# Interleaving the two token halves in the last output group of a decoder-layer kernel

## The chip, the cores and the metric

The kernel runs on one core of a Trainium2 chip. The metric is the device time of one execution in microseconds. The core has a matrix engine (TensorE, here PE), a vector engine (VectorE, DVE), a scalar engine (ScalarE, ACT), GpSimd (POOL), and SyncE (SP), which here issues transfers. Each engine takes its instructions in the order in which they stand in its own list, and waits at an instruction until the semaphores named there have their counts.

## The reference, cut to what matters

One residual layer over 256 tokens of width 2048: three token-mixer branches, each projected to the model width and merged by gates, then an output projection, the residual, and a final norm. The change is in the last line but one, in a quarter of its columns.

```python
merged = (g_sb * (o_sb @ w_branch_sb[layer])
          + g_ssd * (o_ssd @ w_branch_ssd[layer])
          + g_mem * (o_mem @ w_branch_mem[layer]))
x = x + merged @ w_out[layer]
return rms_norm(x, final_norm_w)     # x / sqrt(mean(x*x) + eps) * final_norm_w
```

## The kernel before

Float32 products are made of three reduced-precision ones: each operand is split into a high and a low part (`split`: ACT makes the high part, line 146; DVE subtracts to get the low part, line 150), and PE adds high x high, high x low and low x high into one accumulator in PSUM. Weights are streamed: `load_chunk` (line 207) has SP load two k-tiles of 128 rows x 512 columns (512 KB) into one of four `raw` buffers, `split` writes `wh` and `wl`, and the matmuls follow. Tokens are 256, in two halves `t` of 128; the halves are the two 128-column slices of the left operand.

The output projection has 2048 columns in four groups of 512, with 16 k-tiles each. Groups 0 to 2 go through `gemm` (lines 266 to 268), which takes both token halves for each k-tile, in an accumulator tile `acc` with one 512-column bank for each half. The tag `acc` has two buffers, taken in turn. What follows a group (`out_half`, line 880: residual add on DVE, then squares on ACT and a product on POOL) is deferred by three chunks of the next `gemm`, so that it doesn't hold up the splits. Group 2 has no `gemm` behind it.

Group 3, the last one, is written out by hand (lines 934 to 953). First its eight chunks are loaded and split into four `wlh` and four `wll` tiles that hold them all (`his`, `los`); then `drain()` issues what was still deferred, which is group 2's `out_half` for both halves; so these stand behind the eight splits on DVE. Then come the products: token half 0 with all 512 columns and 16 k-tiles; its epilogue `last_cols` (lines 892 to 898: residual add, squares, sum, norm weight, for 256 columns at a time) and `write_out` (lines 902 to 912: inverse root on POOL, scaling of the whole row on DVE and ACT, five writes); then token half 1 in two column halves of 256 with 16 k-tiles each, each in an accumulator of its own and each with its `last_cols`, and at the end `write_out`. Engines' lists are in the order of this code: no scheduler moves anything. Waits are derived from which tiles an instruction reads and writes; an accumulator buffer that is taken again waits for the readers of the tile that had it.

Of the kernel before, what the change touches and what calls it, by code (L numbers as in the profile page):

```python
# [10 lines left out]
F32 = mybir.dt.float32  # L11
# [5 lines left out]
P = 128  # L17
D = 2048
T = 256
NKT = D // P  # L20
GW = 512
# [4 lines left out]
LATE = 3  # L26
WARM = 10
LATE_C = 2
NEG = -1.0e30

SB_HEADS = 8
# [10 lines left out]
def trunk_kernel(  # L42
# [6 lines left out]
    nc = tc.nc  # L49
# [7 lines left out]
    psA = ctx.enter_context(tc.tile_pool(name="psA", bufs=2, space=bass.MemoryType.PSUM))  # L57
# [4 lines left out]
    def nm(s):  # L62
        cnt[0] += 1
        return f"{s}_{cnt[0]}"
# [13 lines left out]
    def tq(shape, n):  # L78
        return tmp.tile(shape, F32, tag="tq", name=nm(n), bufs=2)

    def small(shape, n="small"):
        return sm.tile(shape, F32, tag="small", name=nm(n), bufs=12)
# [4 lines left out]
    def bank(shape, n="bank"):  # L87
        return psB.tile(shape, F32, tag="bank", name=nm(n))
# [19 lines left out]
    def keep_warm(n):  # L108
        for _ in range(n):
# [9 lines left out]
    nc.gpsimd.memset(cmask, 0.0)  # L119
    nc.gpsimd.affine_select(out=smask, in_=cmask, compare_op=ALU.is_gt, fill=NEG, base=0,  # L120
                            pattern=[[1, P]], channel_multiplier=-1)
    nc.gpsimd.affine_select(out=cmask, in_=cmask, compare_op=ALU.is_ge, fill=NEG, base=0,
                            pattern=[[1, P]], channel_multiplier=-1)
# [48 lines left out]
    def defer(fn, chunks=LATE):  # L172

        cnt[0] += 1
        heapq.heappush(late, (now[0] + chunks, cnt[0], fn))
# [9 lines left out]
    def pump():  # L185


        now[0] += 1
        while late and late[0][0] <= now[0]:
            heapq.heappop(late)[2]()  # L190
        advance(lanes[now[0] % 2])
# [6 lines left out]
    def drain():  # L198
        while lanes[0] or lanes[1] or late:
            pump()  # L200
# [10 lines left out]
    def gemm_cols(lhs, nk, w, c0, evac, ready=None, acc=None):  # L211
# [7 lines left out]
        for k0 in range(0, nk, KCC):  # L219
# [16 lines left out]
            pump()  # L236
        defer(lambda: evac(acc), LATE_C)

# [201 lines left out]
    for g in range(4):  # L440
        gemm_cols(memT, NKT, w_mem_kv, 2 * g * P, to_split_cols(kT, 2 * g),
                  acc=None if g else [bank([P, 2, T], "acc") for _ in range(2)])
# [384 lines left out]
    mT = []  # L827
# [61 lines left out]
    def last_cols(t, cs, acc, xr):  # L889
        for c in range(cs.start, cs.stop, T):  # L890
            yc = yo[t][:, 3 * GW + c:3 * GW + c + T]
            nc.vector.tensor_tensor(yc, acc[:, c - cs.start:c - cs.start + T], xr[:, c:c + T],
                                    ALU.add)
            junk = tq([P, T], "junk")
            q = ssy[:, t, 3 + c // T:4 + c // T]
            nc.scalar.activation(junk, yc, AF.Square, scale=D ** -0.5, accum_out=q)
            nc.vector.tensor_tensor(msy[:, t:t + 1], q, msy[:, t:t + 1], ALU.add)
            nc.vector.tensor_tensor(yc, yc, fw[:, 3 * GW + c:3 * GW + c + T], ALU.mult)

    def write_out(t):  # L900
        rs = small([P, 1], "frs")
        nc.gpsimd.tensor_tensor(rs, msy[:, t:t + 1], mhalf[:, 0:1], ALU.pow)
        for c0, c1, eng, dma in ((0, 256, nc.vector, nc.sync), (256, 640, nc.scalar, nc.scalar),
                                 (640, 1152, nc.vector, nc.sync),
                                 (1152, 1536, nc.scalar, nc.scalar),
                                 (1536, 2048, nc.vector, nc.sync)):
            o = yo[t][:, c0:c1]
            if eng is nc.vector:
                eng.tensor_scalar(o, o, rs, None, ALU.mult)
            else:  # L910
                eng.activation(o, o, AF.Copy, scale=rs)
            dma.dma_start(out[t * P:(t + 1) * P, c0:c1], o)

    def x_chunk(g):
        xr = t4([P, 2, GW], "xr")
        nc.scalar.dma_start(
            xr, x[:, g * GW:(g + 1) * GW].rearrange("(t p) n -> p t n", p=P))
        return xr
# [9 lines left out]
        gemm(mT[0], NKT, w_out, g * GW, out_evac(g))  # L928


    g = 3
    xr = x_chunk(g)
    his, los = [], []
# [4 lines left out]
        raw = load_chunk(w_out, g * GW, GW, k0, KC)  # L938
        split((his[-1][:, k0 % 4:k0 % 4 + KC], los[-1][:, k0 % 4:k0 % 4 + KC], raw, None))
    drain()  # L940
    for t in range(2):
        tt = slice(t * P, (t + 1) * P)
        for cs in (slice(0, GW),) if t == 0 else (slice(0, T), slice(T, GW)):
            acc = psA.tile([P, 2, GW], F32, tag="acc", name=nm("acc"),
                           bufs=2)[:, 0, 0:cs.stop - cs.start]
            for kt in range(NKT):
                lh, ll = mT[0].at(kt)
                wh, wl = his[kt // 4][:, kt % 4, cs], los[kt // 4][:, kt % 4, cs]
                nc.tensor.matmul(acc, lh[:, tt], wh, start=(kt == 0), stop=False)
                nc.tensor.matmul(acc, lh[:, tt], wl, start=False, stop=False)  # L950
                nc.tensor.matmul(acc, ll[:, tt], wh, start=False, stop=(kt == NKT - 1))
            last_cols(t, cs, acc, xr[:, t])
        write_out(t)


_INS = ['x', 'mem', 'x_cols', 'mem_cols', 'w_cols', 'w_in', 'b_gate', 'dt_bias', 'a_log',
# [39 lines left out]
```

## Time and profile before

| | |
|---|---|
| median of 3 runs | 1229.85 us (1229.75 to 1230.08) |
| the profiled execution | 1229.11 us |
| its span, first to last instruction | 1227.3 us |
| mean granted PE clock | 0.999 |
| PE busy | 1215.8 us |
| PE's first matmul of group 3 | 1195.56 us |
| PE's last matmul ends | 1219.26 us |

In the rows a matmul's name is its accumulator and its operands (`acc<-wlh,mT`), with the moving operand's columns behind (512 or 256). A matmul's duration includes its way through the array and overlaps the next one's, so the rate is read from start to start. PEld are weight loads into the array, which run beside the matmuls.

### The profile page before, as it was taken

Reading aid. Unit: us, or ns where it says so; the run is one execution under the profiler, and the core shown is the slowest. Engines: PE = TensorE matmul, PEld = TensorE weight load, DVE = VectorE, ACT = ScalarE, POOL = GpSimd, SP = SyncE. Lnnn points to the kernel's source line nnn. Section 1 sums busy time; section 2 is a strip of 40 time slices with the busy share of each in tenths; the row PEclk is TensorE's granted clock in tenths of the full one; section 3 lists DMA queues with packets and bytes.
Section 4 is the critical chain, followed back from the end, with each engine's and each line's share of the span. In section 5 each row is a group of like instructions: output and inputs, shape, how many; then the busy total and the mean of one; then the engine's idle time right before and its main releaser. Section 6 shows DMA issues by size and latency. Waiting matters only on the chain.

```text
span 1227.3 us, 16568 instructions
## 1 busy us (share of the span) xinstructions
PE 1215.8 (99%) x6388; PEld 1034.4 (84%) x6388; DVE 784.0 (64%) x990; ACT 645.8 (53%) x873; POOL 51.9 (4%) x50
## 2 busy tenths in 40 slices
PE   9999999999999999999999999999999999999997
PEld 7888888888888888888888888888878888888886
DVE  5686554565654555888888758577677655555554
ACT  6765543554444454545665756484757544444443
POOL 0000000000000000010100000000000010110101
PEclk9999999999999999999999999999999999999999
DMA  9966566655566656565567666566756666567673
GB/s 341 335 199 189 162 196 189 185 169 164 168 178 184 188 172 180 169 184 173 176 185 228 207 197 215 183 218 189 232 183 189 206 191 210 186 198 240 199 244 110
DMA packets 175023, 242.70 MB, mean 198 GB/s; under 512 B 10272, under 2 KB 109792, under 8 KB 174816
## 3 DMA queue, kind: packets, MB, share of 16 engines
q1 hardware_dynamic: 168656, 230.17, 60.9%
q10 hardware_dynamic: 6288, 11.48, 2.7%
q8 instruction: 50, 0.82, 0.3%
q14 instruction: 29, 0.24, 0.1%
HBM read 239.48 MB, written 2.13 MB: 197 GB/s over the span
## 4 chain that ended last, share of the span: by engine, by line
PE 95%; DMA 1%; ACT 1%; DVE 1%; issue 1%; SPq 0%; POOLq 0%; POOL 0%; ACTq 0%
PE acc L229 29%; PE acc L266 15%; PE acc L233 14%; PE acc L267 14%; PE acc L268 14%; PE acc L401 1%; PE acc L402 1%; PE acc L400 1%; PE y L773 1%; DMA raw<-in_w_out_dram 1%; DMA raw<-in_w_mem_kv_dram 1%; DVE wl L150 0%; ACT wh L146 0%; PE dtp L460 0%; PE xp L731 0%
## 5 line engine op out<-in xcount | busy, mean ns | idle before, releaser
L150 DVE TENSOR_TENSOR wl<-raw,wh 128x1024 fp32r<-128x1024 f32 (+1 forms) x409 | 504.5, 1237 | 310.3 <-ACT wh L146 305.1
L146 ACT ACTIVATE wh<-raw 128x1024 fp32r<-128x1024 f32 (+1 forms) x409 | 431.1, 1055 | 390.9 <-PE acc L268 200.6
L229 PE MATMUL acc<-hT,wh 128*128 128x512 f32 x1408 | 444.0, 397 | 0.0
L233 PEld LDWEIGHTS acc<-hT,wl 128*128 128x128 f32 x1408 | 264.5, 188 | 62.5
L233 PE MATMUL acc<-hT,wl 128*128 128x256 f32 x1408 | 276.8, 278 | 0.0
L229 PEld LDWEIGHTS acc<-hT,wh 128*128 128x128 f32 x1408 | 214.4, 189 | 0.1
L266 PE MATMUL acc<-wh,hT 128*128 128x512 f32 x448 | 175.7, 392 | 0.0
L267 PE MATMUL acc<-wl,hT 128*128 128x512 f32 x448 | 174.6, 390 | 0.7 <-DVE wl L150 0.7
L268 PE MATMUL acc<-wh,hT 128*128 128x512 f32 x448 | 174.5, 390 | 0.0
L267 PEld LDWEIGHTS acc<-wl,hT 128*128 128x128 f32 x448 | 84.2, 188 | 18.1 <-DVE wl L150 1.2
L268 PEld LDWEIGHTS acc<-wh,hT 128*128 128x128 f32 x448 | 84.1, 188 | 17.7
L266 PEld LDWEIGHTS acc<-wh,hT 128*128 128x128 f32 x448 | 84.1, 188 | 17.6 <-issue 0.7
L266 PE MATMUL acc<-wh,oD 128*128 128x512 f32 x128 | 49.8, 389 | 0.0
L267 PE MATMUL acc<-wl,oD 128*128 128x512 f32 x128 | 49.8, 389 | 0.0
L268 PE MATMUL acc<-wh,oD 128*128 128x512 f32 x128 | 49.8, 389 | 0.0
L688 DVE SCALAR_TENSOR_TENSOR cT<-cu,wcols,cT 128x255 f32<-128x255 f32 (+2 forms) x96 | 46.4, 483 | 3.4
L853 POOL TENSOR_TENSOR merged<-merged,sig 128x512 f32<-128x512 f32 x16 | 24.9, 1574 | 522.6 <-DVE sig L852 522.6
L229 PE MATMUL acc<-memT,wh 128*128 128x512 f32 x128 | 40.6, 398 | 0.0
L266 PE MATMUL acc<-wh,mT 128*128 128x512 f32 x96 | 37.4, 390 | 0.0
L268 PE MATMUL acc<-wh,mT 128*128 128x512 f32 x96 | 37.4, 389 | 0.0
L267 PE MATMUL acc<-wl,mT 128*128 128x512 f32 x96 | 37.4, 389 | 0.0
L631 POOL TENSOR_TENSOR lm<-lm,sp 128x384 f32<-128x384 f32 x8 | 13.1, 1642 | 394.7 <-DVE sp L630 385.0
(250 smaller groups left out, 1298.8 us busy)
## 6 DMA issues: line engine op xcount, KB each, us to landing
raw<-in_w_in_dram SPq DMA_DIRECT2D x288, 512.0 KB, 3.8
raw<-in_w_branch_ssd_dram SPq DMA_DIRECT2D x32, 512.0 KB, 4.5
raw<-in_w_out_dram SPq DMA_DIRECT2D x32, 512.0 KB, 5.0
raw<-in_w_mem_kv_dram SPq DMA_DIRECT2D x31, 512.0 KB, 5.7
raw<-in_w_branch_mem_dram SPq DMA_DIRECT2D x16, 512.0 KB, 3.6
raw<-in_w_branch_sb_dram SPq DMA_DIRECT2D x16, 512.0 KB, 4.8
dec<-acT SPq DMA_DIRECT2D x24, 256.0 KB, 8.0
sig<-in_b_gate_dram ACTq DMA_DIRECT2D x12, 256.0 KB, 4.4
```

Of the source, the lines that this page charges most:

```text
L146: nc.scalar.activation(hi, src, AF.Copy, **({} if scale is None else {"scale": scale}))
L150: nc.vector.tensor_tensor(lo, src, h32, ALU.subtract)
L229: nc.tensor.matmul(halves[b], wh[:, kt - k0, b * P:(b + 1) * P], lhs.both(kt), start=first, stop=False, skip_group_check=True)
L233: nc.tensor.matmul(halves[b][:, 1], wl[:, kt - k0, b * P:(b + 1) * P], lhs.at(kt)[0], start=False, stop=last, skip_group_check=True)
L266: nc.tensor.matmul(a, lh[:, tt], wh[:, j], start=first, stop=False)
L267: nc.tensor.matmul(a, lh[:, tt], wl[:, j], start=False, stop=False)
L268: nc.tensor.matmul(a, ll[:, tt], wh[:, j], start=False, stop=last)
L400: nc.tensor.matmul(a, lh[:, tt], wh[:, g], start=first, stop=False)
L401: nc.tensor.matmul(a, lh[:, tt], wl[:, g], start=False, stop=False)
L631: nc.gpsimd.tensor_tensor(lm, lm, sp, ALU.subtract)
L688: nc.vector.scalar_tensor_tensor(a[:, s:T], u[:, 0:T - s], convw[:, 3 - s, i:i + 1], a[:, s:T], ALU.mult, ALU.add)
L853: nc.gpsimd.tensor_tensor(merged[t][:, cs], merged[t][:, cs], sig[:, t], ALU.add)
```

## The change

The last group's products are reordered. For the first eight k-tiles (`BOTH = 8`) PE does both token halves, 512 columns wide, k-tile by k-tile, into two accumulators that are both taken at the start. Then token half 0 finishes its other eight k-tiles, with its epilogue and `write_out(0)`. Then token half 1 does its other eight k-tiles for the first 256 columns, with their `last_cols`, and for the second 256 columns, both in the one accumulator of token half 1.

```diff
-    for t in range(2):
+
+    accs = [psA.tile([P, 2, GW], F32, tag="acc", name=nm("acc"), bufs=2) for _ in range(2)]
+
+    def products(t, cs, k0, k1, ends=False):
         tt = slice(t * P, (t + 1) * P)
-        for cs in (slice(0, GW),) if t == 0 else (slice(0, T), slice(T, GW)):
-            acc = psA.tile([P, 2, GW], F32, tag="acc", name=nm("acc"),
-                           bufs=2)[:, 0, 0:cs.stop - cs.start]
-            for kt in range(NKT):
-                lh, ll = mT[0].at(kt)
-                wh, wl = his[kt // 4][:, kt % 4, cs], los[kt // 4][:, kt % 4, cs]
-                nc.tensor.matmul(acc, lh[:, tt], wh, start=(kt == 0), stop=False)
-                nc.tensor.matmul(acc, lh[:, tt], wl, start=False, stop=False)
-                nc.tensor.matmul(acc, ll[:, tt], wh, start=False, stop=(kt == NKT - 1))
-            last_cols(t, cs, acc, xr[:, t])
-        write_out(t)
+        for kt in range(k0, k1):
+            lh, ll = mT[0].at(kt)
+            wh, wl = his[kt // 4][:, kt % 4, cs], los[kt // 4][:, kt % 4, cs]
+            for i, (a, b) in enumerate(((lh, wh), (lh, wl), (ll, wh))):
+                nc.tensor.matmul(accs[t][:, 0, cs], a[:, tt], b, start=(kt == 0 and i == 0),
+                                 stop=(ends and kt == k1 - 1 and i == 2),
+                                 skip_group_check=True)
+
+    everything = slice(0, GW)
+    for kt in range(BOTH):
+        for t in range(2):
+            products(t, everything, kt, kt + 1)
+    products(0, everything, BOTH, NKT, ends=True)
+    last_cols(0, everything, accs[0][:, 0], xr[:, 0])
+    write_out(0)
+    for cs in (slice(0, T), slice(T, GW)):
+        products(1, cs, BOTH, NKT, ends=True)
+        last_cols(1, cs, accs[1][:, 0, cs], xr[:, 1])
+    write_out(1)
```

PE's list at the start of group 3, before. The number behind a name is that of the tile; `acc_1841` is token half 0's accumulator. Each chunk's first high part waits for ACT, its first low part for DVE.

```order
L949 MATMUL acc_1841_10153<-wlh_1821_10099,mT_1515_8525 128x512 [waits Activation_49]
L950 MATMUL acc_1841_10153<-wll_1822_10100,mT_1515_8525 128x512 [waits DVE_49]
L951 MATMUL acc_1841_10153<-wlh_1821_10099,mT_1515_8525 128x512
L949 MATMUL acc_1841_10153<-wlh_1821_10099,mT_1515_8525 128x512
L950 MATMUL acc_1841_10153<-wll_1822_10100,mT_1515_8525 128x512
L951 MATMUL acc_1841_10153<-wlh_1821_10099,mT_1515_8525 128x512
L949 MATMUL acc_1841_10153<-wlh_1821_10099,mT_1515_8525 128x512 [waits Activation_49]
L950 MATMUL acc_1841_10153<-wll_1822_10100,mT_1515_8525 128x512 [waits DVE_49]
```

And now, the same place from the third matmul on (all products are line 952 in the changed file); `acc_1842` is token half 1's accumulator.

```order
L952 MATMUL acc_1841_10153<-wlh_1821_10099,mT_1515_8525 128x512
L952 MATMUL acc_1842_10154<-wlh_1821_10099,mT_1515_8525 128x512 [waits DVE_49]
L952 MATMUL acc_1842_10154<-wll_1822_10100,mT_1515_8525 128x512
L952 MATMUL acc_1842_10154<-wlh_1821_10099,mT_1515_8525 128x512
L952 MATMUL acc_1841_10153<-wlh_1821_10099,mT_1515_8525 128x512
L952 MATMUL acc_1841_10153<-wll_1822_10100,mT_1515_8525 128x512
L952 MATMUL acc_1841_10153<-wlh_1821_10099,mT_1515_8525 128x512
L952 MATMUL acc_1842_10154<-wlh_1821_10099,mT_1515_8525 128x512
L952 MATMUL acc_1842_10154<-wll_1822_10100,mT_1515_8525 128x512
L952 MATMUL acc_1842_10154<-wlh_1821_10099,mT_1515_8525 128x512
L952 MATMUL acc_1841_10153<-wlh_1821_10099,mT_1515_8525 128x512 [waits Activation_49]
L952 MATMUL acc_1841_10153<-wll_1822_10100,mT_1515_8525 128x512
```

Token half 1's first product is now the fourth of the group and has a wait on DVE; the low parts of the later chunks have none any more.

PE's list where token half 1 goes from its first 256 columns to the second, before (two accumulators, `acc_1845` and `acc_1847`):

```order
L949 MATMUL acc_1845_10224<-wlh_1833_10129,mT_1518_8528 128x256
L950 MATMUL acc_1845_10224<-wll_1834_10130,mT_1518_8528 128x256
L951 MATMUL acc_1845_10224<-wlh_1833_10129,mT_1518_8528 128x256
L949 MATMUL acc_1847_10278<-wlh_1821_10099,mT_1515_8525 128x256 [waits DVE_49,PE_49]
L950 MATMUL acc_1847_10278<-wll_1822_10100,mT_1515_8525 128x256
L951 MATMUL acc_1847_10278<-wlh_1821_10099,mT_1515_8525 128x256
```

Now (one accumulator, `acc_1842`; x2 stands for two rows alike):

```order
L952 MATMUL acc_1842_10154<-wlh_1833_10129,mT_1518_8528 128x256 x2
L952 MATMUL acc_1842_10154<-wll_1834_10130,mT_1518_8528 128x256
L952 MATMUL acc_1842_10154<-wlh_1833_10129,mT_1518_8528 128x256
L952 MATMUL acc_1842_10154<-wlh_1829_10119,mT_1517_8527 128x256 [waits DVE_49]
L952 MATMUL acc_1842_10154<-wll_1830_10120,mT_1517_8527 128x256
```

Before, the wait was for the readers of token half 0's accumulator; now it stands between two column halves of the same tile.

DVE's list at that place now. Apart from the tiles' numbers it is the list of before; line 910 is `write_out(0)`, line 893 the residual add of `last_cols`.

```order
L910 TENSOR_SCALAR yo_1726_9616<-yo_1726_9616,frs_1845_10237 128x256 [waits Pool_49]
L910 TENSOR_SCALAR yo_1726_9616<-yo_1726_9616,frs_1845_10237 128x512
L910 TENSOR_SCALAR yo_1726_9616<-yo_1726_9616,frs_1845_10237 128x512 [waits DVE_49]
L893 TENSOR_TENSOR yo_1727_9617<-acc_1842_10154,xr_1820_10097 128x256 [waits PE_49]
L898 TENSOR_TENSOR msy_9621<-ssy_9620,msy_9621 128x1 [waits Activation_49]
L899 TENSOR_TENSOR yo_1727_9617<-yo_1727_9617,fw_1728_9618 128x256 [waits DVE_49]
L893 TENSOR_TENSOR yo_1727_9617<-acc_1842_10154,xr_1820_10097 128x256 [waits PE_49]
```

The scalings of token half 0 stand ahead of both reads of token half 1's accumulator, as they did; what moved is the matmuls around them.

More of the change, by code (lines that the diff above doesn't have):

```diff
@@ L28 @@
 LATE_C = 2
+BOTH = 8
 NEG = -1.0e30
```

## The prediction

> **What bounds the kernel now.** I read the page first, then the rows of the last 40 us, engine by engine, since the change touches only the last of the four output groups. The page says that TensorE (PE) sets the time:
>
> ```profile
> span 1227.3 us, 16568 instructions
> PE 1215.8 (99%) x6388; PEld 1034.4 (84%) x6388; DVE 784.0 (64%) x990; ACT 645.8 (53%) x873; POOL 51.9 (4%) x50
> PE 95%; DMA 1%; ACT 1%; DVE 1%; issue 1%; SPq 0%; POOLq 0%; POOL 0%; ACTq 0%
> ```
>
> The chain that ended last is PE for 95% of the span, so a hole in PE is paid in full unless work behind it gets shorter. Here are PE's rows around the last group (start, duration, engine, line; in square brackets the idle time before a row and who ended it). Line 268 is the end of group 2; lines 949 to 951 are the last group.
>
> ```profile
> 1195.33 0.39 PE L268 MATMUL acc<-wh,mT 128*128 128x512 f32 x1
> 1195.56 0.39 PE L949 MATMUL acc<-wlh,mT 128*128 128x512 f32 x1
> 1195.78 0.39 PE L950 MATMUL acc<-wll,mT 128*128 128x512 f32 x1
> 1196.01 0.39 PE L951 MATMUL acc<-wlh,mT 128*128 128x512 f32 x1
> 1196.24 0.39 PE L949 MATMUL acc<-wlh,mT 128*128 128x512 f32 x1
> ...
> 1206.24 0.39 PE L951 MATMUL acc<-wlh,mT 128*128 128x512 f32 x1
> 1207.49 0.38 PE L949 MATMUL acc<-wlh,mT 128*128 128x256 f32 x1 [0.86 <-DVE yo L880]
> 1207.71 0.28 PE L950 MATMUL acc<-wll,mT 128*128 128x256 f32 x1
> ...
> 1213.22 0.28 PE L951 MATMUL acc<-wlh,mT 128*128 128x256 f32 x1
> ...
> 1218.98 0.28 PE L951 MATMUL acc<-wlh,mT 128*128 128x256 f32 x1
> ```
>
> From start to start a 512-column matmul takes (1206.24 - 1195.56) / 47 = 0.227 us, and a 256-column one (1218.98 - 1207.71) / 94 = 0.120 us. Token half 0 is 48 of the first, token half 1 two times 48 of the second. After the last matmul (1218.98 + 0.28 = 1219.26) the span has 8.04 us left: the last epilogue, the writes and the end of the program. PE is without a hole in the group except one, in front of token half 1, and that one was ended by VectorE's line 880, the residual add of group 2. VectorE (DVE) at that place:
>
> ```profile
> 1189.83 2.35 DVE L150 TENSOR_TENSOR wll<-raw,wlh 128x1024 fp32r<-128x1024 f32 x2
> ...
> 1203.88 1.23 DVE L150 TENSOR_TENSOR wll<-raw,wlh 128x1024 fp32r<-128x1024 f32 x1 [1.46 <-ACT wlh L146]
> 1205.02 0.68 DVE L880 TENSOR_TENSOR yo<-acc,xr 128x512 f32<-128x512 f32 x1
> 1206.75 0.68 DVE L880 TENSOR_TENSOR yo<-acc,xr 128x512 f32<-128x512 f32 x1
> ...
> 1208.49 0.42 DVE L892 TENSOR_TENSOR yo<-acc,xr 128x256 f32<-128x256 f32 x1
> ...
> 1211.97 1.15 DVE L909 TENSOR_SCALAR yo<-yo,frs 128x256 f32<-128x256 f32 x3 [0.45 <-POOL frs L902]
> 1213.54 0.42 DVE L892 TENSOR_TENSOR yo<-acc,xr 128x256 f32<-128x256 f32 x1 [0.43 <-PE acc L951]
> ...
> 1219.30 0.42 DVE L892 TENSOR_TENSOR yo<-acc,xr 128x256 f32<-128x256 f32 x1 [4.18 <-PE acc L951]
> ```
>
> What to see: group 2's products are complete at about 1195.7, but its adds run at 1205.02 and 1206.75, because in VectorE's order the eight weight splits of the last group (1189.83 to 1205.1) stand ahead of them. The second add ends at 1207.43 and PE goes on 0.06 later. Why the splits take so long is in the waits of the window from 1170 on: ScalarE waits for the weights' transfers, not for PE.
>
> ```profile
> ACT wlh L146 <- DMA raw<-in_w_out_dram: 6.9, 6, 2.2
> DVE wll L150 <- ACT wlh L146: 5.4, 4, 2.0
> ```
>
> So the two adds come at about 1207 whatever PE does in this group: nothing on that path (transfer, ScalarE, VectorE) waits for the last group's matmuls.
>
> **Term 1, the wait that moves: +11.25 us.** The pool has two accumulators that take turns. The first one of the last group is group 1's, free long ago; the second is group 2's. Before, PE asks for the second one after 48 matmuls of cover, at 1206.24 + 0.23 = 1206.47. Now it asks after three, as matmul number four, at 1196.24. The order of the changed kernel puts a wait on VectorE on that matmul, and the waits on VectorE that each later chunk's `wll` had are gone, which says that the new wait is for a point behind all eight splits, as the adds are. PE is in order, so everything stands behind it: the remaining products of both halves. It resumes as before at 1207.49: 1207.49 - 1196.24 = 11.25 us of hole. Nothing hides it; the cover was the 45 products of token half 0 that now stand behind the wait.
>
> **Term 2, the hole of before: -1.02 us.** PE's idle slot from 1206.47 to 1207.49 is the same wait, and is not paid twice.
>
> **Term 3, wider matmuls: -0.32 us.** The first eight k-tiles of token half 1 are now 24 matmuls of 512 columns in place of 48 of 256: 24 x 0.227 = 5.44 us against 48 x 0.120 = 5.76.
>
> **Term 4, the clock: +2.35 us.** After 11 us without a matmul the clock is not at full speed. Rows of the start of the program (the first matmuls after idleness), and windows whose third column from the right is the granted clock:
>
> ```profile
> 1.06 4.63 PE L110 MATMUL warm<-ones 128*128 128x128 f32 x20 [1.06 <-POOL ones L99]
> 5.56 0.63 PE L400 MATMUL acc<-wh,memT 128*128 128x512 f32 x1
> 6.03 0.39 PE L401 MATMUL acc<-wl,memT 128*128 128x512 f32 x1
> 6.62 0.39 PE L400 MATMUL acc<-wh,memT 128*128 128x512 f32 x1
> 1206.60:1207.50 0.90, 0.04 (x2) 0.01 (x1) 0.80 (x3) 0.03 (x1) 0.90 (x1) 1.00 0.00 0
> 1223.00:1224.00 1.00, 0.00 (x0) 0.00 (x0) 0.00 (x0) 0.00 (x0) 0.00 (x0) 1.00 1.02 383
> 1224.00:1225.00 1.00, 0.00 (x0) 0.00 (x0) 0.00 (x0) 0.00 (x0) 0.00 (x0) 0.71 1.01 369
> 1225.00:1226.00 1.00, 0.00 (x0) 0.00 (x0) 0.00 (x0) 0.00 (x0) 0.00 (x0) 0.50 0.38 118
> ```
>
> The 0.86 us hole of before left the clock at 1.00. After the last matmul it is 1.00 until 1224.0 and 0.50 from 1225.0; a mean of 0.71 puts the fall at 1224.4, 5.2 us after PE went idle. A hole of 11 us is twice that, so PE restarts at half clock. How long it stays there I take from the start: first matmul at 1.06, the one at 5.56 still slow (0.63 against 0.39), the one at 6.03 fast, so it came back 4.5 to 5.0 us after work began. At half rate half of 4.7 us is lost: 2.35 us. The ends: nothing, if the clock stays up as it did over 0.86 us; 2.8 us, if it comes back as late as 5.6 us after work began (by the row at 6.62, from which on each start follows the last by 0.23).
>
> [...]
>
> **Term 5, the second half of token half 1: +2.4 us.** Before, the two 256-column halves were in two different accumulators. Now they are in one, and the order puts a wait on VectorE on the second half's first matmul: it is for line 893 (892 before), the read of the first half. What is queued ahead of that read on VectorE counts, and this is the whole epilogue and scaling of token half 0, which before ran beside 5.8 us of matmuls and now has only 24 x 0.120 = 2.88 us of them. Let X be the start of token half 0's last matmul. VectorE starts 0.39 + 0.04 after it (as at 1219.30 against 1218.98 + 0.28), needs 1211.97 + 1.15 - 1208.49 = 4.63 us up to the end of the three scalings of `write_out(0)`, 0.42 for the read, and PE restarts 0.06 later: X + 5.54. PE is through the first half at X + 0.23 + 2.88 = X + 3.11. Difference 2.4 us. With VectorE free it would still be 0.7 (0.28 + 0.04 + 0.42 + 0.06 after the last start in place of 0.12), which is the low end; nothing else stands ahead of the read, so 2.4 is near the high one.
>
> **What costs nothing.** DVE, ACT, POOL and SP issue the same instructions in the same order as before; only the matmuls move. The five writes of token half 0 come closer to those of token half 1, and the cover for that is time: the scaling that starts them comes at X + 0.43 + (1211.97 - 1208.49) = X + 3.9, that of token half 1 at X + 5.54 + 23 x 0.120 + 0.28 + (1221.25 - 1219.26) = X + 10.6, 6.7 us later (9.3 before), and a write lands 3.0 us after its issue:
>
> ```profile
> 1221.25 1.14 DVE L909 TENSOR_SCALAR yo<-yo,frs 128x256 f32<-128x256 f32 x3 [0.46 <-POOL frs L902]
> out_dram<-yo SPq DMA_DIRECT2D x4, 256.0 KB, 3.0
> ```
>
> So the two sets don't meet, and after the last matmul the tail stays 8.04 us. The weights' waits for token half 1 can't come back, since the splits are done before PE resumes.
>
> **Sum.** 11.25 - 1.02 - 0.32 + 2.35 + 2.4 = 14.66 us. The profiled execution took 1229.11 us, 1.8 above its span, and becomes 1243.8; against the median of the runs shown, 1229.85, it is 1244.5 us, 1.2% slower. (About 0.2%, 2.5 us, is what a measurement of this kernel can tell from no change.)
>
> **Rivals.**
> - *Other side: no hole.* If the second accumulator were free when matmul four asks, terms 1 and 4 vanish: -1.02 - 0.32 + 2.4 = +1.06, so 1230.9 us, no change. For it: group 2's products are done at 1195.7, and two adds take only 1.4 us. Against it: the adds stand behind the splits on VectorE and ended at 1207.43. It decides for "no change" if the second add ends before about 1197.6, ten microseconds earlier than seen. Chance 4%.
> - *The clock stays up* or falls too late to matter: term 4 is zero, 1242.15 us. For it: only the short hole has been seen between matmuls, and that left 1.00. Against it: the fall 5.2 us after the last matmul. Chance 9%.
> - *The clock stays low for the rest of the group.* The 69 wide matmuls after the hole (15.7 us) and the 48 narrow ones (5.8 us) would take twice that: 21.4 us lost in place of 2.35, and 1263 us. Against it: at the start it came back within 5 us under the same kind of work. Chance 3%.
> - *Only the first add gates* (the new accumulator lies where token half 0 of group 2 lay, and that add ended at 1205.70): 1.7 us less, 1242.8 us. For it: the data overlap only there. Against it: before, PE resumed 0.06 after the second add, not after the first. Chance 4%.
>
> **How the numbers follow.** The forecast as written has 80%, with 1243.3 to 1246 as its own range: 2.35 may be 1.4 to 2.8, and the adds shift with the weights' transfers, whose waits were up to 2.2 us each, by half a microsecond or so each way. The range is 1241.5 to 1246.3: it takes in the clock that stays up and the earlier add. Slower by over 0.2%: all cases but the first rival, 95%; same 4%; faster 1%, for what I have not thought of.
>
> **What the changed profile would show.** PE: three matmuls at about 1195.6 to 1196.0, then a hole of about 11 us that ends with a wait for the group-2 add, at about 1207.5. Granted clock 0.50 from about 1201 to 1212, and 512-column matmuls after the hole at about 0.43 from start to start at first. A second hole of about 2.4 us before the last 24 matmuls, ended by the 256-column add. Last matmul about 1233.8, then 8 us. I am wrong if the adds of group 2 come much before 1207 (term 1), if the clock column stays at 1.00 (term 4), or if the second hole is absent (term 5).

## The result, and the profile after

The changed kernel takes 1244.8 us (median of four runs, 1244.02 to 1245.66) against 1229.8 us before: a ratio of 1.0118, 95% interval 1.0106 to 1.0130. It is slower by 15.0 us, and 14.66 were forecast. The profiled execution has a span of 1243.7 us.

```profile
span 1243.7 us, 16519 instructions
PE 1219.6 (98%) x6364; PEld 1036.0 (83%) x6364; DVE 784.1 (63%) x990; ACT 645.6 (52%) x873; POOL 51.9 (4%) x50
```

DVE and ACT have the same work as before, to 0.2 us. PE has 24 matmuls fewer and still 3.8 us more of busy time. Of that, 2.8 us lie in the last group, where the slow clock adds 3.1 by the sum below and the wider matmuls take off 0.3; the rest lies ahead of the group, where the two kernels are alike. PE's rows of the last group, in order of time (all products are line 952 now; x2 merges two neighbours of one form, and `...` marks rows left out):

```profile
1196.49 0.39 PE L952 MATMUL acc<-wlh,mT 128*128 128x512 f32 x1
1196.71 0.39 PE L952 MATMUL acc<-wll,mT 128*128 128x512 f32 x1
1196.94 0.39 PE L952 MATMUL acc<-wlh,mT 128*128 128x512 f32 x1
1208.63 0.79 PE L952 MATMUL acc<-wlh,mT 128*128 128x512 f32 x1 [11.30 <-DVE yo L881]
1209.22 0.63 PE L952 MATMUL acc<-wll,mT 128*128 128x512 f32 x1
...
1225.62 0.51 PE L952 MATMUL acc<-wlh,mT 128*128 128x512 f32 x2
...
1228.60 0.28 PE L952 MATMUL acc<-wlh,mT 128*128 128x256 f32 x1
1231.06 0.39 PE L952 MATMUL acc<-wlh,mT 128*128 128x256 f32 x1 [2.18 <-DVE yo L893]
...
1235.24 0.41 PE L952 MATMUL acc<-wlh,mT 128*128 128x256 f32 x1
```

Two holes, each ended by the add that was named. VectorE's rows say why they end there:

```profile
1205.01 1.22 DVE L151 TENSOR_TENSOR wll<-raw,wlh 128x1024 fp32r<-128x1024 f32 x1 [0.54 <-ACT wlh L147]
1206.15 0.68 DVE L881 TENSOR_TENSOR yo<-acc,xr 128x512 f32<-128x512 f32 x1
1207.89 0.68 DVE L881 TENSOR_TENSOR yo<-acc,xr 128x512 f32<-128x512 f32 x1
...
1226.05 0.42 DVE L893 TENSOR_TENSOR yo<-acc,xr 128x256 f32<-128x256 f32 x1 [16.34 <-PE acc L952]
...
1229.52 1.15 DVE L910 TENSOR_SCALAR yo<-yo,frs 128x256 f32<-128x256 f32 x3 [0.45 <-POOL frs L903]
1230.58 0.42 DVE L893 TENSOR_TENSOR yo<-acc,xr 128x256 f32<-128x256 f32 x1
```

The second group-2 add ends at 1207.89 + 0.68 = 1208.57, behind the last split, and PE resumes 0.06 later. The read of token half 1's first half starts at 1230.58, as soon as the three scalings of token half 0 are through, and not when its products are (1228.88). The granted clock around both holes, in windows of 1 us. Each row has the window, its length, the busy time of PE, PEld, DVE, ACT and POOL, and then the clock, third from the right:

```profile
1200.00:1201.00 1.00, 0.00 (x0) 0.00 (x0) 0.91 (x2) 0.76 (x1) 0.00 (x0) 1.00 0.79 291
1201.00:1202.00 1.00, 0.00 (x0) 0.00 (x0) 1.00 (x1) 0.00 (x0) 0.00 (x0) 0.73 0.78 270
1202.00:1203.00 1.00, 0.00 (x0) 0.00 (x0) 0.02 (x1) 0.90 (x1) 0.00 (x0) 0.50 0.38 139
...
1211.00:1212.00 1.00, 1.00 (x5) 0.79 (x4) 0.00 (x0) 0.00 (x0) 0.00 (x0) 0.65 0.00 0
1212.00:1213.00 1.00, 1.00 (x6) 0.82 (x5) 0.00 (x0) 0.00 (x0) 0.00 (x0) 1.00 0.00 0
...
1231.00:1232.00 1.00, 0.94 (x8) 0.95 (x9) 0.00 (x0) 0.56 (x3) 0.00 (x0) 1.00 1.02 369
1232.00:1233.00 1.00, 1.00 (x8) 1.00 (x7) 0.49 (x2) 0.14 (x2) 0.00 (x0) 0.59 1.01 389
1233.00:1234.00 1.00, 1.00 (x7) 1.00 (x7) 0.00 (x0) 0.00 (x0) 0.00 (x0) 0.50 0.69 219
```

The first hole brings the fall that was forecast. But the clock falls a second time, at about 1232.2, in the middle of the last 24 matmuls; that was not in the prediction.

The sum, from start to start in these rows:

| term | forecast | measured |
|---|---|---|
| 1 first hole (1208.63 - 1196.94 - 0.23) | +11.25 | +11.46 |
| 2 hole of before, gone | -1.02 | -1.02 |
| 3 24 wide for 48 narrow | -0.32 | -0.32 |
| 4 slow clock behind the first hole (1225.85 - 1208.63 - 69 x 0.227) | +2.35 | +1.56 |
| 5 second hole (1231.06 - 1228.60 - 0.12) | +2.4 | +2.34 |
| slow clock at the end (1235.65 - 1231.06 - 23 x 0.120 - 0.28) | none | +1.55 |
| sum | 14.66 | 15.57 |

Terms 2 and 3 come from the rows of before: the hole is not there again, and outside the slow stretches PE keeps the same 0.227 and 0.120 us from start to start.

From the group's first matmul to the end of the span it is 1243.7 - 1196.49 = 47.2 us against 1227.3 - 1195.56 = 31.7 before: 15.5 us, which the sum meets. (The spans differ by 16.4, because the group starts 0.9 us later in this execution. The code ahead of it is the same. In the ten profiles of after and of the experiments it starts between 1195.45 and 1197.82. Below, profiles are therefore compared by the length from the group's first matmul to the end of the span, called the group's length.)

### The profile page after: what moved, and what is told of

Same layout as the page of the kernel before. It is cut to its first block, busy times and chain, and to the rows that moved or that the text cites. A ratio compares the mean times of both kernels' runs of the same rounds, so it can differ in the third digit from the quotient of the medians.

```text
span 1243.7 us, 16519 instructions
## 1 busy us (share of the span) xinstructions
PE 1219.6 (98%) x6364; PEld 1036.0 (83%) x6364; DVE 784.1 (63%) x990; ACT 645.6 (52%) x873; POOL 51.9 (4%) x50
## 4 chain that ended last, share of the span: by engine, by line
PE 93%; DMA 3%; ACT 1%; DVE 1%; issue 1%; SPq 0%; POOLq 0%; POOL 0%; ACTq 0%
PE acc L230 29%; PE acc L267 14%; PE acc L234 14%; PE acc L268 14%; PE acc L269 14%; PE acc L952 1%; DMA rows<-in_mem_dram 1%; DMA raw<-in_w_mem_kv_dram 1%; PE y L774 1%; DMA raw<-in_w_out_dram 1%; PE acc L402 0%; PE acc L403 0%; PE acc L401 0%; DVE wl L151 0%; ACT wh L147 0%
## 5 line engine op out<-in xcount | busy, mean ns | idle before, releaser
L952 PE MATMUL acc<-wlh,mT 128*128 128x512 f32 (+1 forms) x80 | 23.8, 382 | 13.5 <-DVE yo L881 11.3
```

Source lines behind the costliest of these rows:

```text
L952: nc.tensor.matmul(accs[t][:, 0, cs], a[:, tt], b, start=(kt == 0 and i == 0), stop=(ends and kt == k1 - 1 and i == 2), skip_group_check=True)
```

## The experiments

Nine kernels, each one edit away from the changed kernel, from the one before, or from another experiment. The ratios are to the kernel before on the same chip. Hole 1 is the one ahead of token half 1's first product, hole 2 the one ahead of its second 256 columns. The last three columns are of the profiled execution alone. A to F are the theories that the expectations name.

| kernel | ratio, 95% interval | group's length | idle in hole 1 / hole 2 | clock below 1.00 ahead of the last matmul |
|---|---|---|---|---|
| before | 1 | 31.7 | 0.86 / none | no |
| changed | 1.0118 (1.0106 to 1.0130) | 47.2 | 11.30 / 2.18 | twice |
| e1 own bank | 1.0014 (1.0005 to 1.0024) | 34.2 | none / 2.17 | at the end |
| e2 adds early | 1.0031 (1.0017 to 1.0045) | 34.8 | 1.83 / 2.18 | no |
| e3 first hole filled | 1.0096 (1.0079 to 1.0113) | 45.6 | 1.37 left / 2.17 | at the end |
| e4 before, one bank | 1.0006 (0.9997 to 1.0015) | 32.5 | 0.83 / 0.52 | no |
| e5 own bank, late write | 1.0000 (0.9991 to 1.0009) | 31.1 | none / 0.58 | no |
| e6 both holes filled | 1.0101 (1.0088 to 1.0115) | 44.1 | 1.12 left / 0.33 left | no |
| e7 before, own banks | 0.9990 (0.9981 to 0.9999) | 30.6 | none / none | no |
| e8 two own banks | 1.0000 (0.9991 to 1.0009) | 31.5 | none / none | no |
| e9 as e8, late write | 0.9992 (0.9983 to 1.0002) | 30.7 | none / none | no |

**Is the first hole the accumulator's hand-over?** e1 takes away what makes PE wait: another bank, with no order changed.

```diff
-    accs = [psA.tile([P, 2, GW], F32, tag="acc", name=nm("acc"), bufs=2) for _ in range(2)]
+    accs = [psA.tile([P, 2, GW], F32, tag="acc", name=nm("acc"), bufs=2),
+            bank([P, 1, GW], "acc1")]
```

> The changed kernel, with token half 1's accumulator in a PSUM bank of the other pool, which was free long before; all orders stay. Theory A (the first hole is the hand-over of group 2's accumulator, 11.46 us, and costs 1.56 us of slow clock behind it): both vanish, 1244.8 - 11.5 - 1.6 = 1231.7 us, and up to 1.5 less (1230.2) if the second slow stretch at the very end does not come either. The second hole of about 2.3 us stays. Rival B (PE would have waited anyway for the weights' low parts, which come over 11 us, and the accumulator only names the wait): the hole breaks up into waits for ACT and DVE splits and the time stays above 1240 us.

Measured: 1.0014, 1.7 us over before, where A had up to 1.9 (1231.7 on 1229.8). The first hole is gone, and with it its fall of the clock; no wait for weights takes its place, so B falls. PE's rows of e1 at the second hole, which stays:

```profile
1214.99 0.28 PE L953 MATMUL acc<-wlh,mT 128*128 128x256 f32 x1
1217.44 0.39 PE L953 MATMUL acc<-wlh,mT 128*128 128x256 f32 x1 [2.17 <-DVE yo L893]
```

And e1's windows behind it, with the granted clock third from the right, which falls again:

```profile
1217.00:1218.00 1.00, 0.56 (x4) 0.56 (x5) 0.38 (x2) 0.58 (x1) 0.00 (x0) 1.00 0.86 302
1218.00:1219.00 1.00, 1.00 (x8) 1.00 (x7) 0.44 (x2) 0.51 (x2) 0.00 (x0) 0.63 1.02 381
```

e2 keeps the changed accumulators and moves only the adds in VectorE's list:

```diff
         raw = load_chunk(w_out, g * GW, GW, k0, KC)
+        if k0 == 3 * KC:
+            drain()
         split((his[-1][:, k0 % 4:k0 % 4 + KC], ...))
```

> The changed kernel, with group 2's deferred adds issued after the third of the eight weight splits in place of after the eighth; the accumulators stay as changed. Theory A (the place of the adds in VectorE's list sets the hole): the second add ends at about 1198.3 to 1200 on the clock of the profile before, so the first hole is 2.2 to 3.5 us in place of 11.5, the clock does not fall in it, and the time is 1233 to 1236 us. Rival B (it is the splits themselves that PE waits for): the splits end about 3 us later than now, so the time is 1244 to 1248 us. Risk to A: the splits behind the adds come later than PE wants them, seen as waits for DVE in the later k-tiles.

Measured: 1.0031, a median of 1234.5 us, inside A's 1233 to 1236 and 9 us or more under B's. The first hole is 2.0 us (1200.27 - 1198.27, where PE would have gone on), a little under A's 2.2 to 3.5. The adds and PE in e2:

```profile
1197.79 0.69 DVE L881 TENSOR_TENSOR yo<-acc,xr 128x512 f32<-128x512 f32 x1 [1.87 <-PE acc L269]
1199.53 0.68 DVE L881 TENSOR_TENSOR yo<-acc,xr 128x512 f32<-128x512 f32 x1
...
1200.27 0.50 PE L954 MATMUL acc<-wlh,mT 128*128 128x512 f32 x1 [1.83 <-DVE yo L881]
```

The adds follow group 2's last product at once, PE resumes 0.06 after the second one (1200.21), and the splits behind them, now ending at 1209.6, stop PE nowhere. The place of two adds in one engine's list is worth 9.5 us of hole here (2.0 us in place of 11.46). The group's length falls by 12.4 us, since both slow stretches (1.56 and 1.55 us) go with it: in this execution of e2 the clock does not fall before the last matmul.

**Is the slow start behind the hole the clock?** e3 keeps PE busy in the first hole and leaves its end where it is; e6 does so in both. The extra products go into a spare bank and are used by nothing.

```diff
+    spare = bank([P, GW], "spare")
+
+    def fill(n):
+        for _ in range(n):
+            nc.tensor.matmul(spare, mT[0].at(0)[0][:, 0:P], his[0][:, 0], start=True, stop=True)
+
     for kt in range(BOTH):
         for t in range(2):
             products(t, everything, kt, kt + 1)
+            if kt == t == 0:
+                fill(44)
 ...
     for cs in (slice(0, T), slice(T, GW)):
         products(1, cs, BOTH, NKT, ends=True)
+        if cs.start == 0:
+            fill(8)                      # e6 alone
```

> The changed kernel, with 44 extra matmuls of 512 columns (10 us, into a spare bank, read by nobody) between the third and the fourth matmul of the group, so that PE is busy through most of the first hole but resumes at the same moment. Theory A (the slow start after the hole is the clock, 1.56 us): granted clock 1.00 through the hole, 1244.8 - 1.5 = 1243.3 us if the second slow stretch at the end still comes. Rival C (a restart costs what it costs, and the clock has nothing to do with it): 1244.8 us, unchanged.

> The changed kernel with PE kept busy in both holes: 44 extra matmuls of 512 columns in the first and 8 (1.8 us) in the second, into a spare bank. The holes' ends stay where they are. Theory A (1.56 us behind the first hole and 1.55 us at the end are the clock): no clock below 1.00 before the last matmul, 3.1 us less than the changed kernel, 1241.7 us or a ratio to before of 1.0095; the last 24 matmuls 0.12 us apart in place of 0.21. [...] Rival C (no clock in it): 1.0118.

Measured: the group's length falls from 47.2 to 45.6 with the first hole filled and to 44.1 with both, 1.6 and 3.1 us less, which is what A expected of each. (0.2 of the 3.1 us is that the first hole of e6 ended that much earlier after the group's start, 11.94 us against 12.14.) The times point the same way, 1.0096 and 1.0101 against 1.0118, but their intervals don't tell e3 from e6, and both overlap the changed kernel's; what shows the gain is the rows. The clock column of e6 is 1.00 up to the last matmul. In e3 PE resumes at full rate, and so does e6 behind both of its fills:

```profile
1209.91 0.50 PE L952 MATMUL acc<-wlh,mT 128*128 128x512 f32 x1 [1.37 <-DVE yo L881]
1210.24 0.39 PE L952 MATMUL acc<-wll,mT 128*128 128x512 f32 x1
```

```profile
1230.73 0.38 PE L952 MATMUL acc<-wlh,mT 128*128 128x256 f32 x1 [0.33 <-DVE yo L893]
...
1233.58 0.28 PE L952 MATMUL acc<-wlh,mT 128*128 128x256 f32 x1
```

In the changed kernel the second product behind the first hole came 0.59 us after the first and the last 24 took 4.59 us; here it is 0.33 and 1233.86 - 1230.73 = 3.13. C falls.

**Is the second hole the shared accumulator, or what is queued ahead of the read?** e4 shares one accumulator tile, in one bank, in the order of before; e5 takes e1 and moves the writes of token half 0 behind the read.

```diff
     for t in range(2):
+        whole = psA.tile([P, 2, GW], F32, tag="acc", name=nm("acc"), bufs=2)
         for cs in (slice(0, GW),) if t == 0 else (slice(0, T), slice(T, GW)):
-            acc = psA.tile(...)[:, 0, 0:cs.stop - cs.start]
+            acc = whole[:, 0, cs]
```

> The kernel before, with one edit: token half 1's two column halves share one accumulator tile, side by side in one bank, as in the changed kernel. Token half 1 is not interleaved, so the first half has 5.8 us of matmuls, beside which VectorE gets through with token half 0's epilogue. Theory A (the second hole is the wait for the read of the first half, 0.7 us with VectorE free, and the rest of the 2.3 us is the epilogue queued ahead of the read): a hole of 0.7 us, 1229.8 + 0.7 = 1230.5 us. Rival D (sharing the bank itself costs the 2.3 us): 1232.1 us. Rival E (it does not wait at all, as the columns differ): 1229.8 us.

```diff
     last_cols(0, everything, accs[0][:, 0], xr[:, 0])
-    write_out(0)
     for cs in (slice(0, T), slice(T, GW)):
         products(1, cs, BOTH, NKT, ends=True)
         last_cols(1, cs, accs[1][:, 0, cs], xr[:, 1])
+        if cs.start == 0:
+            write_out(0)
```

> As the run with token half 1's accumulator in a bank of its own (ratio to before 1.0014, second hole 2.2 us idle), but write_out(0) is issued after the read of token half 1's first half, so that the read has only token half 0's epilogue ahead of it on VectorE. Theory A (the epilogue and the scalings queued ahead of the read make the second hole): start of the read at X + 0.43 + 3.0, hole 0.8 us in place of 2.4, so 1.5 us less than that run, and the clock does not fall at the end, up to 1.5 us less again: a ratio to before of 0.999 to 1.0005. Rival D (the shared bank alone makes it): 1.0014, hole unchanged.

PE of e4 where the first half's products end, and then PE of e5 where the second half starts:

```profile
1214.63 0.28 PE L951 MATMUL acc<-wlh,mT 128*128 128x256 f32 x1
1215.42 0.39 PE L949 MATMUL acc<-wlh,mT 128*128 128x256 f32 x1 [0.52 <-DVE yo L892]
```

```profile
1217.15 0.39 PE L953 MATMUL acc<-wlh,mT 128*128 128x256 f32 x1 [0.58 <-DVE yo L893]
```

e4: 1215.42 - 1214.63 - 0.12 = 0.67 us, and the group's length grows by 0.8. So PE does wait, though the two halves have no column in common (E's zero is inside the time's interval, but not in the rows), and with VectorE free the wait is the 0.7 us that term 5 had as its low end. The wait is a semaphore in PE's list, which the program has because both halves are one tile. No run puts two tiles into one bank, so it is not shown whether sharing the bank alone would cost anything. e5: idle 0.58 in place of 2.17, and the clock doesn't fall; 3.1 us less in the group's length than e1, and 1.0014 became 1.0000. D falls: some 1.6 of the 2.3 us are the queue on VectorE (2.17 - 0.58).

**What is the interleaving worth without the two waits?** e7 gives the kernel before the spare banks; e8 gives them to the changed order, one for each column half from the start.

```diff
-            acc = psA.tile([P, 2, GW], F32, tag="acc", name=nm("acc"),
-                           bufs=2)[:, 0, 0:cs.stop - cs.start]
+            acc = bank([P, GW], "acc1")[:, 0:cs.stop - cs.start] if t else psA.tile(
+                [P, 2, GW], F32, tag="acc", name=nm("acc"), bufs=2)[:, 0]
```

> The kernel before, with token half 1's two accumulators in banks of the other pool, which are free; no order changes. Theory A (the 1.0 us hole of the kernel before is the same hand-over of group 2's accumulator): no hole in the group, 1.0 us less, ratio 0.9992. If something else ends at 1207.5 as well: 1.0000. This would be the version that beats both.

Measured: 0.9990, and PE goes from token half 0 to token half 1 without a gap in e7:

```profile
1206.37 0.39 PE L951 MATMUL acc<-wlh,mT 128*128 128x512 f32 x1
1206.59 0.28 PE L949 MATMUL acc<-wlh,mT 128*128 128x256 f32 x1
```

This version beats both kernels: against the kernel before it is 1.1 us shorter in the group's length and 1 us in the time, whose interval just excludes 1.

```diff
-    accs = [psA.tile([P, 2, GW], F32, tag="acc", name=nm("acc"), bufs=2) for _ in range(2)]
+    acc0 = psA.tile([P, 2, GW], F32, tag="acc", name=nm("acc"), bufs=2)
+    halves = [bank([P, T], "acc1") for _ in range(2)]
 ...
     for kt in range(BOTH):
-        for t in range(2):
-            products(t, everything, kt, kt + 1)
+        products(0, everything, kt, kt + 1)
+        for cs in (slice(0, T), slice(T, GW)):
+            products(1, cs, kt, kt + 1)
```

> The changed kernel's interleaving, with token half 1's two column halves in two banks of the other pool from the start (so all its products are 256 columns wide, 96 of them as before). Theory A (the interleaving as such costs and brings nothing; the two waits do it all): no hole, 1.0 us less than before, ratio 0.9992, the same as with the order of before. Rival F (the interleaving itself costs, by weights that come too late for it or by the epilogue of token half 0 that ends beside fewer matmuls): a ratio over 1.000, with waits of PE for ACT or DVE in the first eight k-tiles or a longer tail.

A missed here. There is no hole in PE, but the ratio is 1.0000, and from the last matmul's end to the end of the span it is 1226.9 - 1218.07 = 8.8 us, not 8.0. F was right in its second part. (The interval still takes in A's 0.9992; the rows decide.) The last matmul and the last add of e8:

```profile
1217.79 0.28 PE L954 MATMUL acc<-wlh,mT 128*128 128x256 f32 x1
...
1218.90 0.42 DVE L893 TENSOR_TENSOR yo<-acc,xr 128x256 f32<-128x256 f32 x1
```

The add comes 0.83 us after its products. The cover for the epilogue of token half 0 has shrunk from two halves of 5.8 us to two of 2.9, and VectorE arrives late. e9 is e8 with the move of e5:

> The interleaving with two banks for token half 1, and write_out(0) issued after the epilogue of token half 1's first half. In the run without that move, the last add came 0.8 us after its products, since VectorE was still at the first half's epilogue, which had waited for ScalarE's scaling of token half 0; from the last matmul's end to the end of the span it was 8.8 us in place of 8.0. If that queue is the cause: the last add follows the last matmul by 0.04 us unless the scalings of token half 0, which now come later, hold it; 8.0 us behind the last matmul, 30.6 us from the group's first matmul to the end, ratio 0.999. If it is not: 8.8 and 31.4 us, ratio 1.000.

```profile
1218.13 0.28 PE L954 MATMUL acc<-wlh,mT 128*128 128x256 f32 x1
...
1218.45 0.42 DVE L893 TENSOR_TENSOR yo<-acc,xr 128x256 f32<-128x256 f32 x1 [0.21 <-PE acc L954]
```

The add is 0.04 us behind its products again, the tail is 8.0 us, and the group's length is 30.7, as in e7 (30.6): the queue on VectorE was what made e8's tail longer. So the interleaving as such brings nothing here; it needs two accumulators in free banks and another order of the epilogues to be no worse than the order of before with free banks.

## Why the prediction was right, and where it was off

- **Term 1, the first hole: right**, in cause and size (11.46 for 11.25). e1 takes it away with another bank, e2 shrinks it by moving the adds alone. PE resumed after the second add, so the rival by which only the first gates fell. So did the rival without a hole.
- **Terms 2 and 3** came as written. e7 shows term 2 apart from all else: 1.1 us shorter without the hand-over.
- **Term 4, the clock: the mechanism was right, its size was not.** It was 1.56 us, not 2.35, by the rows, and e3 gets 1.6 back. The clock was back 3.1 us after PE resumed (the 0.65 of the window from 1211 puts it at 1211.7), not after the 4.7 that I took from the start of the program. So both rivals on the clock fell: it did drop, and it did come back. The step that failed is that one duration from one place was taken for another.
- **Term 5, the second hole: right** (2.34 for 2.4), and so was its split into the wait on the shared accumulator (0.7, e4) and the queue ahead of the read (the rest, e5).
- **A term was missing:** the second hole lowered the clock too, for the last 24 matmuls, +1.55 us in the profiled execution. The prediction had the 0.86 us hole as evidence that short holes leave the clock alone, and put no clock term beside term 5. With term 4 too large by 0.79 and this one left out, the sum was 0.9 us too small in the profile; that the medians differ by only 0.3 us from the forecast owes something to luck.
- **What costs nothing: right for the changed kernel.** Its tail is 1243.7 - 1235.65 = 8.05 us as before (8.04). In e8, without the holes, VectorE was late for the last add and the tail was 8.8.

## What to carry to other kernels

Before an accumulator is taken earlier, find who read its buffer last and where that read stands in its engine's list: here two adds of 0.7 us, deferred behind eight weight splits, cost 11 us. Two column halves in one accumulator tile that are written and read in turn waited for each other here, though they share no column: 0.67 us in e4, where VectorE was free, and 2.34 us in the changed kernel, with token half 0's epilogue and scalings queued ahead of the read. Price a hole in PE with the clock behind it: the 2.3 us hole cost 1.55 us more in the profiled execution of the changed kernel, and nothing more in that of e2.

## What the runs showed of the hardware that was not expected

A hole of 2.2 us lowered the clock in three profiles of four. It fell in the changed kernel (2.18 us idle), e1 (2.17) and e3 (2.17), 1.1, 0.8 and 1.4 us after PE had resumed, and it did not in e2 after a hole of the same length (2.18): there the clock column is 1.00 up to 1226.0, and PE's last matmul ended at 1224.39. Nor did it take one length of idle time to fall. In the first hole of the changed kernel the fall came 4.1 us after the third matmul's end at 1197.33 (the 0.73 of the window from 1201 puts it at 1201.46), in the kernel before 5.2 us after the last matmul's end (1224.4 - 1219.26), and in e4 2.0 us after it. The windows of e4 around its end:

```profile
1221.00:1222.00 1.00, 0.43 (x4) 0.23 (x2) 0.42 (x1) 0.07 (x1) 0.00 (x0) 1.00 0.00 0
1222.00:1223.00 1.00, 0.00 (x0) 0.00 (x0) 0.49 (x2) 0.44 (x2) 0.29 (x1) 1.00 0.00 0
1223.00:1224.00 1.00, 0.00 (x0) 0.00 (x0) 0.58 (x2) 0.58 (x1) 0.39 (x1) 0.69 0.00 0
```

The 0.69 puts the fall at 1223.38, and PE worked until 1221.43. What sets the moment of the fall was not shown: no run moved a hole on purpose.

The timed executions do point to a hole of 2.2 us lowering the clock in some executions of a kernel and not in others. The profiled executions of e1 and e3, which have the fall, have a mean clock of 0.997, and that of e2, which has none ahead of its last matmul, 0.998. In all, 7 of 10 executions of e1, 3 of 6 of e2 and 2 of 4 of e3 have 0.996 or 0.997, and they are longer than the others of their kernel by 1.0, 1.9 and 2.9 us in the mean. In e4 to e9, which have no hole of that length left at the end, none of 56 is below 0.998, and of the kernel before 2 of 61 are (0.997). So the 1.55 us at the end look like a cost that comes and goes between executions, which a single profile can't tell.
